# The activation of SwiGLU, turned between two matmuls: by transposing DMA of halfword planes instead of TensorE

## The chip, the cores and the metric

One core of one Trainium2 chip runs the whole program. The metric is the device time of one execution in microseconds (us), the median of several executions. The engines are named as in the profile: PE (TensorE, matmuls), ACT (ScalarE), DVE (VectorE), POOL (GpSimd) and SP (SyncE, which here only issues DMA). Sixteen DMA engines move data between DRAM and the on-chip memory (SBUF); matmul results land in PSUM, in 8 banks.

## The reference

One layer of a decoder: 256 tokens, width 2048, all in float32. The change lies in the feed-forward part, the last but one of the layer's parts.

```python
D_MODEL = 2048; SEQ = 256; D_FF = 5632
...
x = x + rms_norm(merged @ w_out[layer], g_mix_post[layer])

h = rms_norm(x, g_ffn_pre[layer])
gate, up = jnp.split(h @ w_gate_up[layer], 2, axis=-1)
x = x + rms_norm((jax.nn.silu(gate) * up) @ w_down[layer], g_ffn_post[layer])

ple_gate = jax.nn.sigmoid(rms_norm(x, g_ple_pre[layer]) @ w_ple_gate[layer])
...
```

`silu(gate) * up` is "the activation": 256 tokens by 5632 channels. It comes out of the first matmul with tokens on the partitions, and the second matmul needs it with channels on the partitions, so it has to be turned (transposed) in between.

## The kernel before

**Products.** A float32 product is made of three matmuls of a faster type: each operand is split into a high part, made by a copy on ACT (`wh` of a weight, `hi` of an activation), and the rest, made by a subtraction on DVE (`wl`, `lo`). `terms` issues high by high, low by high and high by low. Some blocks of weights go by "quads": seven products in place of eight, with sums of weights (`t`, made on DVE) and sums of activations (`sides`, split into `shi` and `slo`).

**The feed-forward part.** The 256 tokens are two chunks `c` of 128. `swiglu(j)` makes block `j` (of `NJ` = 11, 512 channels each) of gate and up from `w_gate_up`; `ev_g` and `ev_u` take the sums out of PSUM, and the product of silu(gate) and up is a tile `t` (named `u`, or `sg` for block 0) of 128 tokens by 512 channels. `gated(c, j, t)` then turns it: four PE transposes into a PSUM bank (`misc<-ident,u`), one ACT copy to SBUF (`actT<-misc`), and a store to a DRAM scratch tile `actd[c][j]` from the SP queue. There are 22 such tiles of 256 KB.

The second matmul takes the channels in five groups of blocks (`KGROUPS`), once for the left half of the output's columns and once, backwards, for the right half (`DOWN`). `act_parts(pair, gi)` prepares a group's activation while PE works on the group before: `load(j)` fetches both chunks of a block from `actd` by DMA from the POOL queue, one block ahead of its use, and `split` makes `hi` and `lo` of each. Blocks are loaded again for the second half, except for the group at the turn: 40 loads in 9 groups.

**What sets the order.** Weights are loaded by SP into six buffers `raw`, in a fixed plan. Work beside the matmuls is written as generators ("chains"): each `yield` says after what or after how long the chain may go on, by the planner's own estimate of time, which advances with every matmul that is written. So the order of each engine's instructions is fixed when the program is built; at run time each engine goes through its own list in that order, and waits where an operand or a buffer isn't there. If a matmul is written and its `hi` and `lo` aren't, `hurry` writes the missing steps on the spot:

```python
def hurry(done):
    while not done():
        due, _, gen = heapq.heappop(waiting)
        step(gen, due)
```

Tiles live in 61 equal SBUF slots; `room(n)` holds a chain back until n of them are free. In the estimate, DMA transfers take no time of an engine; `act_parts` leaves 6.0 us between the first load of a group and its use. All recorded instructions carry line 181, that of the recording helper, so the profile's groups go by the tiles' names.

Of the kernel before, what the change touches and what calls it, by code (L numbers as in the profile page):

```python
# [13 lines left out]
F32 = mybir.dt.float32  # L14
F32R = mybir.dt.float32r
I32 = mybir.dt.int32
AF = mybir.ActivationFunctionType
ALU = mybir.AluOpType
AX = mybir.AxisListType

P = 128
D = 2048
NB = 512
DFF = 5632
NJ = DFF // NB
# [4 lines left out]

TABLES = (AF.Sigmoid, AF.Silu, AF.Exp, AF.Ln, AF.Sin)
TABLE_LOAD = 1.3
# [96 lines left out]
def block_kernel(ctx: ExitStack, tc: tile.TileContext, I, out: bass.AP):  # L129
# [24 lines left out]
    class InOrder:  # L154
# [20 lines left out]
        def __getattr__(self, name):  # L175
            f = getattr(self.engine, name)

            def call(o, *a, **kw):
                if name != "dma_start":
                    self.estimate(name, o, a, kw)  # L180
                return tc.keep_in_program_order(f(o, *a, **kw))  # L181

            return call

    V = InOrder(nc.vector, 0.07, 0.00105)
    A = InOrder(nc.scalar, 0.16, 0.0008)
    G, T, S = InOrder(nc.gpsimd, 0.9, 0.002), InOrder(nc.tensor, 0.0, 0.0), InOrder(nc.sync, 0.0, 0.0)
# [9 lines left out]
    def transpose(o, i, idn):  # L197
        clock[0] += SMALL
        T.transpose(o, i, idn)
# [29 lines left out]
    def nm(s):  # L229
        count[0] += 1  # L230
        return f"{s}_{count[0]}"
# [4 lines left out]
    def slot(s, shape=(P, NB), dt=F32):  # L236
        i = free_slots.popleft()
        t = slots.tile(list(shape), dt, tag=f"s{i}", name=nm(s))
        owner[id(t)] = i, t
        return t  # L240

    def free(*tiles):
        for t in tiles:
            free_slots.append(owner.pop(id(t))[0])

    def room(n):

        while len(free_slots) < n:
            yield 0.3
# [13 lines left out]
    def drop(ps):  # L263
        banks.append(bank_of.pop(id(ps))[0])
# [5 lines left out]
    def misc():  # L270
        while len(banks) < 3:
            yield 0.3
        return bank("misc")

    def act(o, i, f, **kw):
        return A.activation(o, i, f, **kw)

    def tt(o, a, b, op):
        return V.tensor_tensor(o, a, b, op)
# [12 lines left out]
    def cols(h, d=P):  # L292
        return slice(h * d, (h + 1) * d)
# [21 lines left out]
    def split_pair():  # L315
# [3 lines left out]
        if isinstance(raw, list):  # L319
            parts = [(slot("wh", dt=F32R), slot("wl", dt=F32R)) for j in range(2)]  # L320
            for (hi, lo), r in zip(parts, raw):
                act(hi, r, AF.Copy)
                tt(lo, r, hi.bitcast(F32), ALU.subtract)
            done = partial(free, *parts[0], *parts[1])
            free(*raw)
        elif len(in_pool) < SPLIT + 1:
            hi = wsplit.tile([P, 2, NB], F32R, tag="wh", name=nm("wh"))
            lo = wsplit.tile([P, 2, NB], F32R, tag="wl", name=nm("wl"))
            act(hi, raw, AF.Copy)
            tt(lo, raw, hi.bitcast(F32), ALU.subtract)  # L330
            parts, done = [(hi[:, j, :], lo[:, j, :]) for j in range(2)], in_pool.popleft
            in_pool.append(k)
        else:
            parts = [(slot("wh", dt=F32R), slot("wl", dt=F32R)) for j in range(2)]
            for j in range(2):
                act(parts[j][0], raw[:, j, :], AF.Copy)
            for j in range(2):
# [4 lines left out]
    def parts_of_pair():  # L342

        w, k, col, raw, _ = loaded.popleft()
        if len(in_pool) <= SPLIT:
            hi = wsplit.tile([P, 2, NB], F32R, tag="wh", name=nm("wh"))
            lo = wsplit.tile([P, 2, NB], F32R, tag="wl", name=nm("wl"))
            in_pool.append(k)
            act(hi, raw, AF.Copy)
            yield  # L350
            tt(lo, raw, hi.bitcast(F32), ALU.subtract)
            parts, done = [(hi[:, j, :], lo[:, j, :]) for j in range(2)], in_pool.popleft
        else:
            parts = [(slot("wh", dt=F32R), slot("wl", dt=F32R)) for j in range(2)]
            for j in range(2):
                act(parts[j][0], raw[:, j, :], AF.Copy)
            yield
# [271 lines left out]
    def lookup(groups):  # L629
        def there(g):  # L630
            return g in groups if isinstance(groups, dict) else len(groups) > g and groups[g] is not None

        def f(k):
            hurry(lambda: there(k // 4))
            hi, lo = groups[k // 4]
            return hi[:, k % 4, :], lo[:, k % 4, :]
        f.groups = groups
        return f
# [17 lines left out]
    def transpose4(src):  # L656
        ps = yield from misc()
        for i in range(4):
            transpose(ps[:, cols(i)], src[:, cols(i)], ident)
        return ps  # L660

    def split(src, to, at):

        yield from room(2)
        hi = slot("hi", (P, 4, P), F32R)
        lo = slot("lo", (P, 4, P), F32R)
        hf = hi.rearrange("p c t -> p (c t)")
        act(hf, src, AF.Copy)
        yield A
        tt(lo.rearrange("p c t -> p (c t)"), src, hf.bitcast(F32), ALU.subtract)  # L670
        to[at] = hi, lo
# [70 lines left out]
    dram = ctx.enter_context(tc.tile_pool(name="dram", bufs=1, space=bass.MemoryType.DRAM))  # L742
# [64 lines left out]
    sinks = amask[:, 256:272]  # L807
    posi = cst.tile([P, 2], I32, name="posi")

# [223 lines left out]
    def hgrn_core(c, g):  # L1033
# [55 lines left out]
        def scores(lev):  # L1089
# [22 lines left out]
            if lev < 5:  # L1112
                V.copy_predicated(
                    right(sc),
                    cmask[:, cols(lev, 64)].rearrange("p (n w) -> p n w", w=w).unsqueeze(1)
                    .broadcast_to([P, 4, nb, w]).bitcast(I32),
                    pv.rearrange("p h (n w) -> p h n w", w=w))
# [446 lines left out]
    collect, _, apply_and_scale = post(gp)  # L1564
# [37 lines left out]
        block("w_out", K16, n * NB, mL, ev_out(n), LAG * (n == 3), n == 3, mixed_used if n == 3 else None)  # L1602


    actd = [[dram.tile([P, NB], F32, name=nm("actd")) for _ in range(NJ)] for _ in range(2)]
    stored, parts, sides, down_sides = [set(), set()], [], {}, {}
    h2T = [lookup(n.groups) for n in norm2]

    def gated(c, j, t):

        pa = yield from transpose4(t)
        free(t)
        yield T
        at = slot("actT")
        act(at, pa, AF.Copy)
        drop(pa)
        S.dma_start(actd[c][j], at)
        free(at)
        stored[c].add(j)

    def swiglu(j):
        sg, us = [None, None], []

        def ev_g(c, ps):
            def f():
                if j in BY_QUADS and SEVEN:
                    t = yield from total(us, 0, c, ps)
                    yield V
                    act(t, t, AF.Silu, scale=norm2[c].r)
                else:  # L1630
                    yield from norm2[c].ready()
                    t = slot("sg")
                    act(t, ps, AF.Silu, scale=norm2[c].r)
                    drop(ps)
                sg[c] = t
            chain(f())

        def ev_u(c, ps):
            def f():
                if j in BY_QUADS and SEVEN:  # L1640
                    t = yield from total(us, 1, c, ps)
                    while sg[c] is None:
                        yield 0.3
                    yield sg[c]
                    stt(t, t, norm2[c].r, sg[c], ALU.mult, ALU.mult)
                    free(sg[c])
                else:
                    while sg[c] is None:
                        yield 0.3
                    t = sg[c]  # L1650
                    stt(t, ps, norm2[c].r, t, ALU.mult, ALU.mult)
                    drop(ps)
                yield V
                yield from gated(c, j, t)
            chain(f())

        if j in BY_QUADS:
            order = quads_of_block(j)
            if j == NJ - 1:
                parts.extend(act_parts(0, 0))  # L1660
            by_quads("w_gate_up", [j * NB, DFF + j * NB], order, h2T, sides, [[acc(), acc()] for _ in range(2)],
                     {"left": sum(seven for _, seven in order)}, us, evac=lambda n, c, ps: (ev_g, ev_u)[n](c, ps))
            return
        block("w_gate_up", K16, j * NB, h2T, ev_g, LAG * (j == 0))
        depth[0] = SPLIT
        if j == 0:
            in_quads[0] = True
            chain(sides_of(ALL, lambda c: norm2[c].groups, sides))
        block("w_gate_up", K16, DFF + j * NB, h2T, ev_u)

    def act_parts(pair, gi):
        js = KGROUPS[gi]
        hurry(lambda: all(j in stored[c] for c in range(2) for j in js))
        parts = [{}, {}]

        def load(j):
            ts = [slot("act"), slot("act")]
            for c in range(2):
                G.dma_start(ts[c], actd[c][j])
            return ts  # L1680

        def f():
            yield from room(2)
            ts = load(js[0])
            yield 6.0
            for at, j in enumerate(js):
                yield from room(2)
                now, ts = ts, load(js[at + 1]) if at + 1 < len(js) else None
                for c in range(2):
                    yield from split(now[c], parts[c], j)  # L1690
                    yield 0.5
                for i in range(2):
                    wanted = 2 * j + i in SEVEN_DOWN[pair] or (gi == 4 and 2 * j + i in SEVEN_DOWN[1])
                    if wanted and 2 * j + i not in down_sides:
                        a = [t.rearrange("p (c t) -> p c t", c=4)[:, 2 * i + k, :] for t in now for k in range(2)]
                        down_sides[2 * j + i] = yield from in_place_of_quad(*a)
                    yield 0.5
                free(*now)
                yield 2.0
        chain(f())  # L1700
        return parts

# [9 lines left out]
    collect, apply, _ = post(gp)  # L1712
    for at, (pair, gi) in enumerate(DOWN):
# [3 lines left out]
        js = KGROUPS[gi]  # L1717
# [137 lines left out]
```

## Time and profile before

| | |
|---|---|
| median of 3 runs | 1489.03 us (1486.18 to 1490.61) |
| profiled execution, its own time | 1489.56 us |
| its span on the core | 1487.5 us |
| PE busy | 1469.5 us, 99% |
| DVE busy | 1239.9 us, 83% |
| ACT busy | 888.9 us, 60% |
| POOL busy | 62.9 us, 4% |
| DMA | 314.59 MB, mean 211 GB/s |
| granted clock | 0.997 |

Around the span lie 2.06 us of the profiled execution. The product with `w_gate_up` runs from about 705 to 1152 us of the span, the one with `w_down` from there to about 1361 us; its activation is loaded and split from 1102 us on. In a line of the profile, "tile<-tiles" are outputs and inputs by the program's names, "x22" is a count, and "[2.66 <-PE acc L181]" is how long the engine was idle ahead of the row and who ended that.

### The profile page before, as it was taken

The numbers are of one execution on the slowest core, as the hardware profiler recorded it, in microseconds if no ns is written. First come the engines' busy times: TensorE is split into PE (matmuls) and PEld (weight loads), VectorE is DVE, ScalarE is ACT, GpSimd is POOL, SyncE is SP. The second block draws the span as 40 slices with busy tenths as digits, with TensorE's granted clock in tenths as the row PEclk, the third lists the DMA queues.
The fourth block names the chain that finished last, engine by engine and source line by source line (L and its number), as shares of the span: only waits on it lengthen the run. The fifth ranks groups of instructions, "written<-read, shape, count | busy, mean of one in ns | idle before, by whom it ended". The sixth has DMA issues, their size and how long they took to land.

```text
span 1487.5 us, 19958 instructions
## 1 busy us (share of the span) xinstructions
PE 1469.5 (99%) x6838; PEld 1216.3 (82%) x6838; DVE 1239.9 (83%) x2043; ACT 888.9 (60%) x1417; POOL 62.9 (4%) x107
## 2 busy tenths in 40 slices
PE   9999999999999999999999999999999999999997
PEld 6888888888887888888888888888888887888885
DVE  6878958755999867977899999999988899997773
ACT  7755655566666645665655666565655666575661
POOL 2100000000000100000000000000000000010000
PEclk9999999999999999999999999999999999999998
DMA  9754544345576856866756676576677678797551
GB/s 342 257 188 155 171 141 128 114 128 170 184 240 227 309 185 201 272 227 199 252 182 219 205 238 213 174 230 206 215 239 268 214 252 270 214 336 260 192 188 56
DMA packets 159557, 314.59 MB, mean 211 GB/s; under 512 B 11072, under 2 KB 11520, under 8 KB 159456
## 3 DMA queue, kind: packets, MB, share of 16 engines
q1 hardware_dynamic: 153024, 293.38, 61.0%
q0 software_dynamic: 6256, 19.88, 3.7%
q8 instruction: 53, 0.87, 0.2%
q14 instruction: 48, 0.39, 0.1%
q10 hardware_dynamic: 176, 0.07, 0.0%
HBM read 298.08 MB, written 15.21 MB: 211 GB/s over the span
## 4 chain that ended last, share of the span: by engine, by line
PE 64%; DVE 4%; issue 2%; DMA 1%; ACT 1%; DVEq 0%; POOLq 0%; POOL 0%; ACTq 0%
PE acc L181 63%; DVE wl L181 2%; PE misc L181 1%; DVE u L181 1%; ACT wh L181 1%; DVE t L181 1%; DMA raw<-in_w_in 1%; DMA raw<-in_w_down 0%; DMA raw<-in_w_gate_up 0%; DVE eg L181 0%; DVE slo L181 0%; DVE lo L181 0%; ACT hi L181 0%; DVE sides L181 0%; DVE s L181 0%
## 5 line engine op out<-in xcount | busy, mean ns | idle before, releaser
L181 PE MATMUL acc<-wh,hi 128*128 128x512 f32 x1769 | 700.2, 396 | 3.6 <-DVE u L181 2.4
L181 DVE TENSOR_TENSOR wl<-raw,wh 128x1024 fp32r<-128x1024 f32 (+1 forms) x606 | 595.7, 1007 | 115.4 <-ACT wh L181 113.8
L181 PE MATMUL acc<-wl,hi 128*128 128x512 f32 x1769 | 690.0, 390 | 0.0
L181 PE MATMUL acc<-wh,lo 128*128 128x512 f32 x1769 | 688.9, 389 | 0.0
L181 ACT ACTIVATE wh<-raw 128x1024 fp32r<-128x1024 f32 (+1 forms) x606 | 514.3, 883 | 239.8 <-PE acc L181 101.6
L181 PEld LDWEIGHTS acc<-wl,hi 128*128 128x128 f32 x1769 | 332.0, 188 | 71.2 <-DVE wl L181 1.1
L181 PEld LDWEIGHTS acc<-wh,hi 128*128 128x128 f32 x1769 | 332.3, 188 | 70.6 <-DVE u L181 3.2
L181 PEld LDWEIGHTS acc<-wh,lo 128*128 128x128 f32 x1769 | 332.5, 188 | 66.6 <-issue 0.2
L181 ACT ACTIVATE wh<-t 128x512 fp32r<-128x512 f32 x236 | 145.6, 628 | 106.6 <-DVE t L181 85.9
L181 DVE TENSOR_TENSOR wl<-t,wh 128x512 fp32r<-128x512 f32 x236 | 152.2, 683 | 0.5 <-PE acc L181 0.5
L181 DVE TENSOR_TENSOR u<-acc,u 128x512 f32<-128x512 f32 x132 | 86.3, 684 | 18.8 <-PE acc L181 17.6
L181 PE MATMUL acc<-wh,shi 128*128 128x512 f32 x236 | 91.9, 390 | 1.2 <-ACT shi L181 1.2
L181 PE MATMUL acc<-wh,slo 128*128 128x512 f32 x236 | 91.9, 390 | 0.2 <-DVE slo L181 0.2
L181 PE MATMUL acc<-wl,shi 128*128 128x512 f32 x236 | 91.8, 389 | 0.0
L181 DVE TENSOR_TENSOR t<-raw,t 128x512 f32<-128x512 f32 x118 | 81.1, 687 | 3.7
L181 PEld LDWEIGHTS acc<-wh,shi 128*128 128x128 f32 x236 | 44.3, 188 | 10.8 <-ACT shi L181 1.6
L181 PEld LDWEIGHTS acc<-wh,slo 128*128 128x128 f32 x236 | 44.3, 188 | 9.7 <-DVE slo L181 0.5
L181 PEld LDWEIGHTS acc<-wl,shi 128*128 128x128 f32 x236 | 44.3, 188 | 9.2
L181 POOL DMA_DIRECT2D act<-actd x40 | 21.4, 538 | 601.9 <-DVE wl L181 402.4
L181 DVE TENSOR_TENSOR t<-raw,raw 128x512 f32<-128x512 f32 x59 | 40.3, 684 | 3.9 <-DMA raw<-in_w_gate_up 1.9
L181 DVE TENSOR_TENSOR t<-raw 128x512 f32<-128x512 f32 x59 | 40.3, 684 | 0.0
L181 DVE TENSOR_TENSOR lo<-act,hi 128x512 fp32r<-128x512 f32 x40 | 27.2, 684 | 8.1 <-ACT hi L181 8.0
(214 smaller groups left out, 852.1 us busy)
## 6 DMA issues: line engine op xcount, KB each, us to landing
raw<-in_w_gate_up SPq DMA_DIRECT2D x176, 512.0 KB, 4.6
raw<-in_w_in SPq DMA_DIRECT2D x152, 512.0 KB, 4.3
raw<-in_w_down SPq DMA_DIRECT2D x88, 512.0 KB, 5.5
raw<-in_w_out SPq DMA_DIRECT2D x32, 512.0 KB, 5.5
raw<-in_w_ple_gate SPq DMA_DIRECT2D x32, 512.0 KB, 5.1
act<-actd POOLq DMA_DIRECT2D x40, 256.0 KB, 5.6
raw<-in_w_attn_branch SPq DMA_DIRECT2D x16, 512.0 KB, 5.2
raw<-in_w_hgrn_branch SPq DMA_DIRECT2D x16, 512.0 KB, 5.1
```

Source lines behind the costliest of these rows:

```text
L181: return tc.keep_in_program_order(f(o, *a, **kw))
```

## The change

The PE transposes, their PSUM banks and the ACT copy out of PSUM go. In their place `gated` has ACT copy the float32 tile, seen as 1024 halfwords (16 bits), into two planes: all low halfwords, then all high ones (`halves`). The planes go to `actd`, untransposed. On the way back, `load` issues a transposing DMA of 16-bit elements from the ACT queue, 128 by 1024 halfwords into 128 x 8 x 128 (`turned`): four squares of 128 by 128 for each plane, each turned. A second ACT copy (`act<-turned`) interleaves the two planes again into a float32 tile, on which `split` then works as before.

```diff
             def call(o, *a, **kw):
-                if name != "dma_start":
+                if not name.startswith("dma_start"):
                     self.estimate(name, o, a, kw)
...
-    actd = [[dram.tile([P, NB], F32, name=nm("actd")) for _ in range(NJ)] for _ in range(2)]
+    actd = [[dram.tile([P, 2 * NB], U16, name=nm("actd")) for _ in range(NJ)] for _ in range(2)]
...
+    def halves(t):
+
+        return t.bitcast(U16).rearrange("p (n two) -> p two n", two=2)
+
     def gated(c, j, t):

-        pa = yield from transpose4(t)
+        at = slot("halves", (P, 2 * NB), U16)
+        act(at.rearrange("p (two n) -> p two n", two=2), halves(t), AF.Copy)
         free(t)
-        yield T
-        at = slot("actT")
-        act(at, pa, AF.Copy)
-        drop(pa)
         S.dma_start(actd[c][j], at)
         free(at)
         stored[c].add(j)
...
                 yield V
-                yield from gated(c, j, t)
+                gated(c, j, t)
...
         def load(j):
-            ts = [slot("act"), slot("act")]
+            ts = [slot("turned", (P, 8, P), U16) for _ in range(2)]
             for c in range(2):
-                G.dma_start(ts[c], actd[c][j])
+                A.dma_start_transpose(ts[c], actd[c][j])
             return ts
...
             for at, j in enumerate(js):
                 yield from room(2)
-                now, ts = ts, load(js[at + 1]) if at + 1 < len(js) else None
+                turned, ts = ts, load(js[at + 1]) if at + 1 < len(js) else None
+                now = []
                 for c in range(2):
+                    yield from room(3)
+                    now.append(slot("act"))
+                    act(halves(now[c]), turned[c].rearrange("p (two c) t -> p two (c t)", two=2), AF.Copy)
+                    free(turned[c])
+                    yield A
                     yield from split(now[c], parts[c], j)
```

Numbers at the end of a name count the tiles in the order in which the code makes them, over all engines.

PE, at the end of a block of `w_gate_up`, before: the activation `u` of both chunks is turned between two matmuls.

```order
L181 MATMUL acc_10653<-wh_10468,lo_6378 128x512
L181 MATMUL acc_10653<-wl_10469,hi_6377 128x512
L181 MATMUL misc_10669<-ident,u_10188 128x128 x4
L181 MATMUL misc_10674<-ident,u_10186 128x128 x4
L181 MATMUL acc_10654<-wh_10468,hi_6507 128x512
L181 MATMUL acc_10654<-wh_10468,lo_6508 128x512
```

After the change no row of that kind (`misc` from `u` or `sg` of a block) is left on PE: 88 transposes are gone, and the `acc` rows follow each other.

ACT, at the first group of loads (about 1107 to 1113 us of the span), before; the loads themselves stand on POOL, in a list of their own.

```order
L181 ACTIVATE wh_10642<-t_10640 128x512
L181 ACTIVATE actT_10679<-misc_10669 128x512
L181 ACTIVATE actT_10685<-misc_10674 128x512
L181 ACTIVATE u_10604<-u_10604,rest_6726 128x512
L181 ACTIVATE u_10602<-u_10602,rest_6592 128x512
L181 ACTIVATE hi_10709<-act_10649 128x512
```

The same place on ACT after:

```order
L182 ACTIVATE wh_10581<-t_10579 128x512
L182 DMA_TRANSPOSE turned_10583<-actd_6422 128x8x128
L182 DMA_TRANSPOSE turned_10584<-actd_6433 128x8x128
L182 DMA_TRANSPOSE turned_10624<-actd_6423 128x8x128
L182 DMA_TRANSPOSE turned_10625<-actd_6434 128x8x128
L182 ACTIVATE u_10537<-u_10537,rest_6726 128x512
L182 ACTIVATE u_10535<-u_10535,rest_6592 128x512
L182 ACTIVATE act_10637<-turned_10583 128x2x512
L182 ACTIVATE halves_10643<-u_10536 128x1024
```

The loads have moved into ACT's list, and the copy that waits for the first of them stands two instructions behind them.

ACT, at the last block that is prepared (about 1345 to 1357 us), before: between one `hi` of the activation and the next stand four or five other copies.

```order
L181 ACTIVATE hi_13113<-act_13042 128x512
L181 ACTIVATE u_13119<-acc_12332 128x512
L181 ACTIVATE wh_13127<-raw_13037 128x512
L181 ACTIVATE wh_13129<-raw_13037 128x512
L181 ACTIVATE wh_13144<-raw_13053 128x1024
L181 ACTIVATE hi_13152<-act_13043 128x512
```

The same place after:

```order
L182 ACTIVATE act_13152<-turned_12914 128x2x512
L182 ACTIVATE hi_13156<-act_13152 128x512
L182 ACTIVATE wh_13172<-raw_13071 128x1024
L182 ACTIVATE wh_13184<-raw_13098 128x1024
L182 ACTIVATE act_13190<-turned_13081 128x2x512
L182 ACTIVATE hi_13192<-act_13190 128x512
L182 ACTIVATE act_13202<-turned_13082 128x2x512
L182 ACTIVATE hi_13204<-act_13202 128x512
```

Copy and split of one tile stand back to back, as `hurry` writes them; and on PE the matmuls that read these tiles follow without the distance that they had:

```order
L182 MATMUL acc_12175<-wl_12949,hi_13130 128x512
L182 MATMUL acc_12176<-wh_12948,hi_13156 128x512
L182 MATMUL acc_12176<-wh_12948,lo_13157 128x512
L182 MATMUL acc_12176<-wl_12949,hi_13156 128x512
L182 MATMUL acc_12176<-wh_12948,hi_13156 128x512
L182 MATMUL acc_12176<-wh_12948,lo_13157 128x512
L182 MATMUL acc_12176<-wl_12949,hi_13156 128x512
L182 MATMUL acc_12175<-wh_12969,hi_13192 128x512
L182 MATMUL acc_12175<-wh_12969,lo_13193 128x512
```

A chunk's activation is read for six matmuls, then comes the next tile. Counted in the order in which the code writes instructions for all engines, 11 of the 40 `lo` tiles now stand 2 matmuls ahead of the first matmul that reads them; before, none stood closer than 14.

More of the change, by code (lines that the diff above doesn't have):

```diff
@@ L16 @@
 I32 = mybir.dt.int32
+U16 = mybir.dt.uint16
 AF = mybir.ActivationFunctionType
```

## The prediction

> **What bounds the kernel now.** I read the page's engine lines first, then the busy time by stretches for the two stages that the change touches, then PE's waits.
>
> ```profile
> span 1487.5 us, 19958 instructions
> PE 1469.5 (99%) x6838; PEld 1216.3 (82%) x6838; DVE 1239.9 (83%) x2043; ACT 888.9 (60%) x1417; POOL 62.9 (4%) x107
> ```
> ```profile
> 720.00:1165.00 445.00, 444.54 (x2001) 367.63 (x2000) 415.64 (x604) 267.39 (x400) 5.38 (x10) 1.00 0.67 215
> ```
> ```profile
> 1100.00:1360.00 260.00, 258.56 (x1152) 213.71 (x1151) 233.38 (x343) 162.74 (x247) 21.38 (x40) 1.00 0.77 257
> ```
> ```profile
> PE acc L181 <- ACT shi L181: 1.2, 1, 1.2
> PE acc L181 <- DVE slo L181: 0.2, 1, 0.2
> ```
>
> The columns of the two stretches are length, then busy time of PE, PE's weight loads, DVE, ACT and POOL, then clock, DMA share and GB/s. PE is busy for 444.54 of 445 us while the activation is made, and for 258.56 of 260 while it is loaded, split and used; the last rows are all that PE waits for in the second. So PE sets the time: a microsecond taken off PE is gained, and any wait of PE is lost whole. DVE stands next (93% and 90%), then ACT (60% and 63%). What counts is whether ACT and DVE stay ahead of PE after the change.
>
> **Off PE: the transposes.** They are seen between two matmuls:
>
> ```profile
> 1109.47 0.39 PE L181 MATMUL acc<-wl,hi 128*128 128x512 f32 x1
> 1109.70 1.03 PE L181 MATMUL misc<-ident,u 128*128 128x128 f32 x8
> 1110.50 0.48 PE L181 MATMUL acc<-wh,hi 128*128 128x512 f32 x1
> 1110.82 0.40 PE L181 MATMUL acc<-wh,lo 128*128 128x512 f32 x1
> 1111.05 0.40 PE L181 MATMUL acc<-wl,hi 128*128 128x512 f32 x1
> ```
>
> Matmuls start 0.23 us apart (1110.82 to 1111.05). Eight transposes hold the start of the next matmul for 1110.50 - 1109.70 = 0.80 us, and the step behind it is 0.32 in place of 0.23: 0.89 us for both chunks of a block, 11 blocks, **-9.8 us**, all of it on the path. DVE then has its 415.64 us in 435 (96%). Nothing is added to it there, so I take no loss.
>
> **On ACT, making the activation.** 22 copies out of PSUM become 22 copies of 1024 halfwords. The nearest row for these is the copy of 1024 elements:
>
> ```profile
> L181 ACT ACTIVATE actT<-misc x22: 578/597/602, 731.5 to 1160.9; 128x512 f32<-128x512 f32 x22
> ```
> ```profile
> L181 ACT ACTIVATE wh<-raw 128x1024 fp32r<-128x1024 f32 x63 | 65.2, 1053 | 61.6 <-DMA raw<-in_w_down 37.2 <-PE acc L181 24.3
> L181 ACT ACTIVATE hi<-act 128x512 fp32r<-128x512 f32 x40 | 24.3, 617 | 1.3 <-PE acc L181 1.3
> ```
>
> 22 x (1.053 - 0.597) = 10 us more on ACT, of which 6 fall into the second stretch (2.7 us). ACT is idle for 178 of 445 us here; cost 0. The stores stay on SP at the same place, and wait for a copy as before.
>
> **On ACT, loading it.** 40 copies `act<-turned` of 1024 halfwords: 40 x 1.053 = 42 us. 40 DMA issues come over from POOL, where they cost nobody anything (it was 4% busy). No row shows the issue of a transposing transfer. The nearest rows are the two plain issues of ACT's own queue, 0.45 and 0.49 us, and for the upper end the slowest issue of an activation's store on SP, 1182 ns:
>
> ```profile
> 0.74 0.45 ACTq L181 DMA_DIRECT2D ident<-in_c_ident  x1
> 1.21 0.49 ACTq L181 DMA_DIRECT2D grow<-in_g_mix_pre  x1
> ```
> ```profile
> L181 SPq DMA_DIRECT2D actd<-actT x22: 319/338/1182, 732.1 to 1161.5; - x22
> ```
>
> Neither end is nearer by its kind, since a plain issue names rows of 2 KB and this one pieces of them; I take the middle, 0.8 us: 32 us (19 to 47). ACT's work in the second stretch becomes 162.7 + 42 + 32 + 2.7 = 239.5 us (226 to 255) of 257 (three of the PE pairs fall into it): 93%, or 88 to 99%.
>
> **The new wait.** Before, POOL waited for the slots and the loads alone. Now the loads stand in ACT's list, at ACT's own place, and behind them in that list stand all the weights' copies `wh`, for which DVE waits, and then PE. The first load of each of the 9 groups stands 27 matmuls (6.1 us) ahead of its first copy. In the trace, ACT came by the same two places like this, at the first and the second group:
>
> ```profile
> 1106.76 0.64 ACT L181 ACTIVATE wh<-t 128x512 fp32r<-128x512 f32 x1
> 1110.34 1.10 ACT L181 ACTIVATE actT<-misc 128x512 f32<-128x512 f32 x2 [2.94 <-PE misc L181]
> 1111.33 1.32 ACT L181 ACTIVATE u<-u,rest 128x512 f32<-128x512 f32 x2
> 1112.56 0.62 ACT L181 ACTIVATE hi<-act 128x512 fp32r<-128x512 f32 x1
> ```
> ```profile
> 1153.47 1.32 ACT L181 ACTIVATE u<-u,rest 128x512 f32<-128x512 f32 x2
> 1154.70 0.61 ACT L181 ACTIVATE wh<-raw 128x512 fp32r<-128x512 f32 x1
> 1155.39 0.64 ACT L181 ACTIVATE wh<-t 128x512 fp32r<-128x512 f32 x1
> 1155.93 1.05 ACT L181 ACTIVATE wh<-raw 128x1024 fp32r<-128x1024 f32 x1
> 1156.88 0.61 ACT L181 ACTIVATE hi<-act 128x512 fp32r<-128x512 f32 x1
> ```
>
> From the end of the row ahead of the loads to the first `hi` it was 5.2 us (1107.4 to 1112.6) and 2.1 us (1154.8 to 1156.9). A transfer of the same bytes took, from issue to landing:
>
> ```profile
> DMA to landing us min/median/max: 3.8/5.6/7.9
> ```
>
> With 5.6 us and the mean distance of 3.7, ACT stands for 1.9 us at each of 9 places, 17 us; with 3.8, nearly none; with 7.9 and 2.1, 52. That brings ACT's demand to 256 of 257 us (226 to 307): just at its limit, with nothing left to catch up with.
>
> **What PE then waits for.** The order shows it: 11 `lo` tiles, in 7 places (both chunks late in 4 of them), stand 2 matmuls (0.45 us) ahead of their reader, because the chain of a block has become longer by a copy per chunk and by the room that it waits for, and `hurry` writes the rest on the spot. Before, the closest stood 14 ahead, and even there little was left:
>
> ```profile
> 1214.70 0.68 DVE L181 TENSOR_TENSOR lo<-act,hi 128x512 fp32r<-128x512 f32 x1
> 1215.30 0.69 DVE L181 TENSOR_TENSOR wl<-t,wh 128x512 fp32r<-128x512 f32 x1
> 1215.90 1.29 DVE L181 TENSOR_TENSOR lo<-act,hi 128x512 fp32r<-128x512 f32 x2
> ```
> ```profile
> 1217.13 0.39 PE L181 MATMUL acc<-wh,hi 128*128 128x512 f32 x1
> 1217.37 0.40 PE L181 MATMUL acc<-wh,lo 128*128 128x512 f32 x1
> ```
>
> The second of the pair of `lo` ended at 1217.19 and was read at 1217.37, although it stood 17 matmuls (3.9 us) ahead of that read: DVE ran 3.7 us later than the order. Tiles that stand 0.45 us ahead make PE wait about 3.2 us by this row. The other way to price it is the chain itself, as if ACT began it just when PE needs it: copy 1.05, `hi` 0.62, `lo` 0.68, less 0.45, that is 1.9 us. Where the second chunk is late too, ACT needs 1.67 us more for it while PE has six matmuls (1.36 us) to do: 0.3 us. 7 x 1.9 + 4 x 0.3 = 14.5 us by the chain, 7 x 3.2 + 1.2 = 23.6 by the row, 0 if ACT runs well ahead of PE. I take 16, near the chain, since PE's own waits give ACT and DVE time to recover between places that lie 5 to 60 us apart.
>
> **Sum.** -9.8 + 16 = +6.2 us on the profiled execution's 1489.56 us: 1495.8. That execution lies 0.5 us above the median of the runs (1489.03), so I forecast **1495.5 us**. With PE's waits at 6 to 28 us this case alone gives 1485 to 1508.
>
> **Rivals.**
>
> *ACT and DVE stay ahead (faster).* For it: PE's cover of split weights is large. ACT once stood for 7.19 us and PE did not wait at all there:
>
> ```profile
> 1183.82 1.06 ACT L181 ACTIVATE wh<-raw 128x1024 fp32r<-128x1024 f32 x1 [7.19 <-DMA raw<-in_w_down]
> ```
>
> With an issue of 0.47 us and a landing within 4, ACT has 226 us of work in 257 and may be some microseconds ahead at the late places. Then PE loses 0 to 5 us and the time is 1479 to 1484. Against it: that cover is one of weights, and the late tiles are the activation's, which have none. It decides at PE waits of 9.8 us in all, where gain and loss are equal.
>
> *ACT becomes the bound (slower still).* If the issue holds ACT for 1.18 us and the landing is 5.6, ACT's demand is 255 + 17 = 272 of 257 us: 15 us more than PE can hide, beside the 14.5 of the chains: 1489.0 - 9.8 + 29.5 = 1508.7. With 7.9 at every first load it is 307, and 1489.0 - 9.8 + 50 = 1529 by ACT's demand alone. Against it: the two plain issues of that queue are less than half as long. It decides where ACT's demand passes 257 us.
>
> *The DMA engines become the bound (slowest).*
>
> ```profile
> q1 hardware_dynamic: 153024, 293.38, 61.0%
> q0 software_dynamic: 6256, 19.88, 3.7%
> ```
>
> A packet of the first queue carries 1.92 KB and takes 0.610 x 16 x 1487.5 / 153024 = 95 ns; one of the second 3.18 KB and 0.037 x 16 x 1487.5 / 6256 = 141 ns. A square of 128 halfwords has rows of 256 bytes, so a transfer would be 1024 pieces, 64 per engine. If a piece takes as long as a packet of the first queue, a transfer holds all engines for 6.1 us and 40 of them for 243 us, in place of 40 x 0.76 = 30 us. The stretch has 0.77 x 260 = 200 us of DMA work; it would have 413, 156 more than PE's 257: 1489 - 9.8 + 156 = 1635. Against it: the two packets lie on a line of some 25 ns and 0.036 ns per byte, by which a piece takes 34 ns and 40 transfers 87 us: 257 us of DMA work, just what PE needs. It decides at 34 ns per piece. [...]
>
> *The change doesn't do what it says.* The order excludes it: the PE rows are gone, and 40 transposing issues stand on ACT.
>
> **Chances.** Forecast 0.48, ahead of PE 0.24, ACT as bound 0.18, DMA as bound 0.08, something else near the old time 0.02. Below 1484.6 or above 1493.5 (0.3%) is about what a measurement of this kernel tells from no change. Slower: 0.31 of the forecast's 0.48, with 0.18 and 0.08, is 0.57. The same: 0.15 of the forecast, 0.02 of the faster case and the 0.02, together 0.19. Faster: 0.22 and 0.02, 0.24. The range of 1480 to 1521 leaves out the DMA case (0.08), the upper end of ACT as bound (0.06) and the lower end of the faster case (0.04).
>
> **What the profile after would show.** Right: no `misc<-ident,u` on PE; the first stretch shorter by about 9 us and still filled by PE; in the second, PE waits of 10 us and more, on `lo<-act,hi` and `hi<-act`, at `lo` tiles of the late blocks; ACT above 85% busy there. Wrong: PE as full as before (then the faster case), or PE waiting for `wl` and `wh` of weights (then ACT or DMA is the bound; the landing time of `turned<-actd` and the DMA share tell which). The forecast falls if ACT runs some 3 us ahead of PE at the late places, or if a transposing issue holds its queue far longer than 1.2 us.

## The result and the profile after

The changed kernel takes 1550.68 us (median of four executions, 1546.59 to 1553.8) beside 1489.21 of the kernel before: a ratio of 1.0415 [1.0387, 1.0443], 61.5 us slower. The forecast was 1495.5 us with a range of 1480 to 1521; the sign was right, the time lies far outside.

The page of the changed kernel (its recording line is 182 now), and PE's clock in fortieths of the span:

```profile
span 1552.0 us, 19730 instructions
PE 1484.4 (96%) x6750; PEld 1219.6 (79%) x6750; DVE 1243.1 (80%) x2044; ACT 944.4 (61%) x1458; POOL 40.9 (3%) x67
PE   9999999999999999999999999999998789677997
PEclk9999999999999999999999999999999799888999
```

Its two stretches, in the same columns as before:

```profile
720.00:1165.00 445.00, 445.00 (x1965) 368.59 (x1964) 418.04 (x607) 283.70 (x408) 0.00 (x0) 1.00 0.71 217
1100.00:1360.00 260.00, 224.78 (x921) 180.24 (x919) 192.60 (x285) 165.41 (x226) 0.00 (x0) 0.92 0.83 205
```

The first stretch is as full of PE work as it was, at full clock. The loss lies in the second: PE works 224.78 of 260 us, not 258.56, and its clock is 0.92, not 1.00. What PE waits for, and what ACT waits for (total, times, longest):

```profile
PE acc L182 <- ACT hi L182: 30.1, 8, 7.2
PE acc L182 <- DVE lo L182: 11.9, 9, 4.7
PE acc L182 <- ACT shi L182: 7.0, 2, 4.8
PE acc L182 <- DVE slo L182: 3.8, 4, 2.8
```
```profile
ACT act L182 <- issue: 24.8, 8, 7.6
ACT wh L182 <- issue: 13.2, 8, 3.4
ACT wh L182 <- DMA raw<-in_w_down: 26.3, 8, 10.8
```

PE waits 52.8 us for the parts of the activation (`shi` and `slo` are those of its sums), where it waited 1.4. ACT, which makes `hi`, stood before its own next instruction with nothing to wait for that the profile shows, "issue". The transfers themselves, and the timeline of ACT at one such place (rows with ACTq are its DMA issues):

```profile
L182 ACTq DMA_TRANSPOSE turned<-actd x40: 1247/1334/6515, 1101.2 to 1405.0; - x40
L182 ACT ACTIVATE act<-turned x40: 1312/1354/1387, 1107.9 to 1428.4; 128x1024 uint16<-128x1024 uint16 x40
DMA to landing us min/median/max: 3.4/8.4/17.6
```
```profile
1315.15 6.51 ACTq L182 DMA_TRANSPOSE turned<-actd  x1
...
1316.42 2.00 ACT L182 ACTIVATE wh<-raw 128x1024 fp32r<-128x1024 f32 x2
1321.69 4.26 ACTq L182 DMA_TRANSPOSE turned<-actd  x1
1326.00 2.53 ACT L182 ACTIVATE act<-turned 128x1024 uint16<-128x1024 uint16 x2 [7.58 <-issue]
...
1331.83 0.61 ACT L182 ACTIVATE hi<-act 128x512 fp32r<-128x512 f32 x1
```
```profile
1332.50 0.79 PE L182 MATMUL acc<-wh,hi 128*128 128x512 f32 x1 [7.15 <-ACT hi L182]
```
```profile
L182 ACT ACTIVATE act<-turned 128x1024 uint16<-128x1024 uint16 x40 | 53.6, 1352 | 32.9 <-issue 24.8 <-PE acc L182 7.0 <-DMA actd<-halves 1.2
```

ACT finishes two copies of weights at 1318.4 and does nothing until 1326.0, while two issues hold its queue one after the other, 6.51 and 4.26 us. PE gets its `hi` from there at 1332.4, and has waited 7.15 us for it. The 40 issues on the timeline, from 1101.15 to 1404.99, add up to 88 us, but not all of that stops ACT: the two copies of 1316.42 ran while the issue of 1315.15 was under way. ACT's idle time that the profile puts down to issues ahead of `act`, `wh` and `u` is 42.8 us, where it was 8.9 before. Four more stops, of 15.3 us together, are put down to PE but end within 0.1 us of the end of an issue. So about 49 of the 88 us stop ACT. The last row is all that ACT stood ahead of the 40 copies: 32.9 us, of which 1.2 end with a transfer.

Behind a stop like this PE's matmuls look as follows, and the clock by 10 us:

```profile
1216.56 0.39 PE L182 MATMUL acc<-wh,slo 128*128 128x512 f32 x1
1216.79 0.39 PE L182 MATMUL acc<-wl,shi 128*128 128x512 f32 x1
1222.97 0.79 PE L182 MATMUL acc<-wh,hi 128*128 128x512 f32 x1 [5.80 <-ACT hi L182]
...
1224.38 0.63 PE L182 MATMUL acc<-wl,hi 128*128 128x512 f32 x1
1224.80 0.63 PE L182 MATMUL acc<-wh,hi 128*128 128x512 f32 x1
1225.23 0.63 PE L182 MATMUL acc<-wh,lo 128*128 128x512 f32 x1
```
```profile
1220.00:1230.00 10.00, 5.00 (x9) 2.90 (x10) 5.68 (x11) 7.57 (x11) 0.00 (x0) 0.50 0.55 142
1230.00:1240.00 10.00, 10.00 (x39) 8.08 (x39) 7.81 (x13) 4.58 (x8) 0.00 (x0) 0.86 0.59 114
```

Ahead of the wait matmuls start 0.23 us apart, behind it 0.42 to 0.43, and the granted clock of those 10 us is 0.50. So a wait like this costs more than its own length. It isn't so behind every wait: in the same kernel the matmuls stay slow behind a wait of 2.81 us (1178.19) and not behind one of 2.82 (1428.57).

### The profile page after: what moved, and what is told of

It is laid out like the page before. It is cut to its first block, busy times and chain, and to the rows that moved or that the text cites. A ratio compares the mean times of both kernels' runs of the same rounds, so it can differ in the third digit from the quotient of the medians.

```text
span 1552.0 us, 19730 instructions
## 1 busy us (share of the span) xinstructions
PE 1484.4 (96%) x6750; PEld 1219.6 (79%) x6750; DVE 1243.1 (80%) x2044; ACT 944.4 (61%) x1458; POOL 40.9 (3%) x67
## 3 DMA queue, kind: packets, MB, share of 16 engines
q10 hardware_dynamic: 42416, 10.56, 5.8%
## 5 line engine op out<-in xcount | busy, mean ns | idle before, releaser
L182 PEld LDWEIGHTS acc<-wh,hi 128*128 128x128 f32 x1769 | 335.8, 190 | 106.1 <-ACT hi L182 33.9
L182 ACT ACTIVATE act<-turned 128x1024 uint16<-128x1024 uint16 x40 | 53.6, 1352 | 32.9 <-issue 24.8
```

## The experiments

Ratios are to the kernel before on the same chip, with their 95% intervals.

**Without the turning.** From the kernel before, the transposes and the copies out of PSUM are taken away; the activation is stored and loaded as it is.

```diff
-        pa = yield from transpose4(t)
+        S.dma_start(actd[c][j], t)
         free(t)
-        yield T
-        at = slot("actT")
-        act(at, pa, AF.Copy)
-        drop(pa)
-        S.dma_start(actd[c][j], at)
-        free(at)
```

> The kernel before without its 88 PE transposes and the 22 copies out of PSUM: the activation is stored as it is and loaded plain from POOL (the turning is left out). It measures the first term of the sum by itself: 9.8 us less, 1476 to 1481 us. If the transposes were hidden on PE or DVE can't follow a faster PE, 1483 to 1489 us.

1479.79 us, 0.9945 [0.9927, 0.9963]: 8.2 us less (5.5 to 10.9). PE's waits for the activation stay at 2.9 us. The term for the transposes holds. All that the change adds is to be counted from here, 1480.

**Plain loads, from POOL and from ACT.** Everything else of the changed kernel stays (its order and its copies of halfwords), and nothing is turned.

```diff
-                A.dma_start_transpose(ts[c], actd[c][j])
+                G.dma_start(ts[c].rearrange("p a b -> p (a b)"), actd[c][j])
```

> The changed kernel with its order, its copies and its SBUF tiles, but the 40 loads are plain DMA issued from POOL, as before the change; the planes come back unturned (this part of the computation is left out). Theory A (ACT is held by the issue of the transposing transfers, 1.3 us and up to 6.5 us each): most of the loss goes, 1490 to 1502 us, PE's waits fall from 53 to under 20 us. Theory B (the recorded order: activation tiles written 2 matmuls ahead of their reader, plus copies of 1.35 us): the loss stays, 1520 to 1550 us, PE's waits 30 us or more. Theory C (pieces of 256 bytes fill the DMA engines, so weights and activation land late): 1490 to 1505 us like A, and weights land in 5.5 us or less; e2 and e3 tell A from C.

> As the run before it, but the 40 plain loads are issued from ACT, at the place where the changed kernel issues its transposing ones (the turning is left out). Theory A: a plain issue holds ACT for 0.5 us in place of 1.3 to 6.5, so 1492 to 1508 us, within 8 us of the run with POOL. Theory B: 1520 to 1550 us. Theory C: as the run with POOL, within 5 us. If it is the place in ACT's list as such that costs (ACT waits there for slots and landings), it comes out 15 us or more above the run with POOL.

From POOL 1509.24 us, 1.0141 [1.0125, 1.0158]; from ACT 1513.72, 1.0171 [1.0156, 1.0186]. PE's waits with POOL, and the issues on ACT:

```profile
PE acc L182 <- ACT hi L182: 15.0, 7, 3.9
PE acc L182 <- DVE lo L182: 5.4, 9, 2.2
PE acc L182 <- DVE slo L182: 0.3, 1, 0.3
```
```profile
L182 ACTq DMA_DIRECT2D turned<-actd x40: 326/390/617, 1103.4 to 1366.5; - x40
```

So 21 us of the loss, 29 above the kernel without turning, come without any transposing transfer, with 20.7 us of PE waits; that a plain load stands in ACT's list adds 4.5 us. The transposing transfer in its place adds 36 (1.0415 less 1.0171). The time from POOL lies above the ranges of theories A and C and below that of B, the one from ACT above that of A and below that of B: none of them explains the loss alone.

**The transposing loads from SP.** `A.dma_start_transpose` becomes `S.dma_start_transpose`.

> The changed kernel with its 40 transposing transfers issued from SP in place of ACT, nothing else changed. Theory A: ACT is free of the issues, 1500 to 1520 us; what is left is weights' loads that stand behind the issues on SP. Theory B: 1535 to 1550 us, since order and copies stay. Theory C: 1545 to 1565 us, as the pieces stay and the weights' loads now also wait behind them.

1525.17 us, 1.025 [1.0235, 1.0265], outside the ranges of all three theories. Of the 41 us between the changed kernel and the plain loads from POOL (1.0415 less 1.0141), 24.5 go with the issue's place on ACT. The issues are no shorter on SP, but there they hold up only other transfers:

```profile
L182 SPq DMA_TRANSPOSE turned<-actd x40: 1231/2522/4903, 1097.4 to 1383.1; - x40
DMA to landing us min/median/max: 3.4/5.8/9.9
```

The other 16 us lie between this kernel and the plain loads from POOL. At least two things differ there: the transfers land later (5.8 us in place of 4.9), and their issues stand in the queue from which the weights are loaded. ACT's waits for weights of `w_down` are 35.6 us here and 16.2 there. Plain loads from SP, which would tell the two apart, weren't tried.

**Half the pieces.** Only the high plane is turned, from ACT and from SP; a copy of the same length puts it into both halves of each word.

```diff
-            ts = [slot("turned", (P, 8, P), U16) for _ in range(2)]
+            ts = [slot("turned", (P, 4, P), U16) for _ in range(2)]
-                A.dma_start_transpose(ts[c], actd[c][j])
+                A.dma_start_transpose(ts[c], actd[c][j][:, NB:])
```

> The changed kernel with half of each transposing transfer: only the high plane of halfwords is turned (512 halfwords of a row, 32 pieces of 256 bytes per engine instead of 64), and the copy behind it writes that plane into both halves of each word, so the low halves of the activation are left out of the result; the copy's length and the order stay. Theory (the cost goes by pieces: their descriptors are written while the issue holds ACT): the issue falls from 1.33 to about 0.75 us, the landing from 8.4 to about 5.5, PE waits 30 to 40 us instead of 53, 1518 to 1535. Rival (the cost is one per transposing transfer, whatever its size): issue and landing stay, 1543 to 1553.

> The same half transfers, issued by SP instead of ACT, so that ACT's list holds no issue. With the whole transfers from SP it was 1525, 16 us above the plain loads of the same order (1509). Theory (those 16 us are the later landing, which goes by pieces): half of them go, 1513 to 1519. Rival (they are a fixed cost of each transposing transfer): 1522 to 1527.

From ACT 1525.13 us, 1.0251 [1.0231, 1.0271]; from SP 1516.43, 1.0192 [1.0165, 1.0218]. Both times are where the cost by pieces put them; from ACT the landing is 5.6 us, as expected, and PE's waits are 29.1, just below the range given. But the issue isn't 0.75 us:

```profile
L182 ACTq DMA_TRANSPOSE turned<-actd x40: 1204/1232/1301, 1100.5 to 1375.0; - x40
```
```profile
L182 SPq DMA_TRANSPOSE turned<-actd x40: 1188/1216/3137, 1098.7 to 1375.7; - x40
DMA to landing us min/median/max: 2.5/4.5/9.3
```

The issue has a floor that hardly falls with the size, 1.25 us for the whole and 1.20 for half from ACT; what goes by size is the tail. With 64 pieces per engine issues took up to 6.5 us, with 32 these rows of ACT end at 1.30, and the sum on the timeline falls from 88 to 50 us. Half of the expectation (a cost by pieces) fits the tail, the rival's half (a cost per transfer) the floor. That descriptors are written while an issue holds its queue, as the expectation has it, is shown by no run.

**The order.** One `yield A` between the copy of halfwords and the split is taken out, so that 2 instead of 11 `lo` tiles stand two matmuls ahead of their readers; with the transposing loads from ACT, from SP, and with plain loads from POOL.

```diff
                     free(turned[c])
-                    yield A
                     yield from split(now[c], parts[c], j)
```

> The changed kernel without the planner's pause between the interleaving copy of a chunk and its split: copy and high part stand back to back on ACT, which changes the order only. Of the 40 low parts 2, not 11, then stand 2 matmuls ahead of their reader, and 5 to 12 us are usual in the second pass. Theory B: PE's waits on the activation fall by half or more, 1500 to 1525 us. Theory A: no instruction and no issue is gone, 1540 to 1551 us. Theory C: 1545 to 1551 us.

> Both of the above: plain loads from POOL (the turning is left out) and no pause between copy and split. What is left against the kernel before: 40 interleaving copies of 1.35 us and 22 of 1.04 us on ACT, no transposes on PE. If order and transposing transfers are all that costs, PE's waits fall under 6 us and it is the gain with little taken off: 1480 to 1490 us. If the copies themselves fill ACT: 1493 to 1505 us, with PE waits above 10 us.

> Transposing transfers issued from SP, and no pause between copy and split. If the two losses add, 1525 - 15 = 1510 us (1503 to 1516). If with ACT free the order has more to spare, 1490 to 1503 us. If the pieces of 256 bytes on the DMA engines are what is left, 1515 us and more, with weights landing later than 5.5 us.

From ACT 1535.34 us, 1.0313 [1.0278, 1.0348]; from SP 1506.48, 1.0127 [1.0114, 1.014]; plain 1495.17, 1.005 [1.0037, 1.0062]. Each is 14 to 18 us below its partner with the changed order. From ACT the time lies between the ranges of the theories, and PE's waits fall by a quarter (52.8 to 39.8 us), not by half; from SP it is where the two losses add; with plain loads it is where the copies themselves were to cost. There PE still waits:

```profile
PE acc L182 <- DVE lo L182: 8.7, 6, 2.6
PE acc L182 <- ACT hi L182: 1.2, 3, 0.9
```

So the late places are real, and they aren't all: some 15 us stay above the kernel without turning.

**Short copies.** In the last kernel, plain with POOL, both copies of 1024 halfwords become copies of 512 words.

```diff
-        act(at.rearrange("p (two n) -> p two n", two=2), halves(t), AF.Copy)
+        act(at.bitcast(F32), t, AF.Copy)
...
-                    act(halves(now[c]), turned[c].rearrange("p (two c) t -> p two (c t)", two=2), AF.Copy)
+                    act(now[c], turned[c].rearrange("p a b -> p (a b)").bitcast(F32), AF.Copy)
```

> The plain loads from POOL without the yield behind the copy (1495.2), and both kinds of copies made plain ones of 512 f32 elements (about 0.6 us instead of 1.35 and 1.04): what is stored isn't split into planes, and nothing is turned. The order of the instructions stays. Theory (what is left above the kernel without turning, 15 us, is ACT's time in the copies, since ACT and DVE have no slack in this stage): most of it goes, 1481 to 1487. Rival (it is the place of the copy in the chain that counts, a step more behind each load, whatever its length): 1491 to 1496.

1482.26 us, 0.9963 [0.995, 0.9976], inside the theory's 1481 to 1487. The copies take 0.62 us instead of 1.35, and PE's waits for `lo` are gone:

```profile
L182 ACT ACTIVATE act<-turned x40: 611/617/622, 1104.2 to 1351.7; 128x512 f32<-128x512 f32 x40
```
```profile
PE acc L182 <- ACT shi L182: 3.1, 1, 3.1
PE acc L182 <- DVE lo L182: 0.3, 1, 0.3
```

But the order didn't stay, as the expectation had it. The planner estimates a copy on ACT at 0.16 us and 0.0008 for each element, so a copy of half the elements changes what it writes when: written out, no `lo` is left 2 matmuls ahead of its reader, and the closest stands 8 ahead. So 13 us (1.005 less 0.9963) go with the length of the copies, directly and by the order that the planner makes of it; the two weren't tried apart. That the chain has a step more costs 2.7 us or nothing: the intervals of this kernel and of the one without turning overlap.

**The copies on POOL.** In the kernel with loads from SP and without the yield, `act(halves(...))` becomes `G.tensor_copy(halves(...))`. This one computes the whole.

> The transposing loads from SP without the yield (1506.5), and the 40 copies that put the halfwords together on POOL instead of ACT; POOL has nothing else to do here. It computes the whole. [...] Theory (ACT's own time in issue and copies makes PE wait): ACT gets 54 us back, PE waits at a few late places only, 1486 to 1496. Rival (the length of the chain load, copy, hi, lo counts at the late places, and POOL's copy is longer): 1504 to 1520.

1526.54 us, 1.0267 [1.0247, 1.0286], 20 us worse than with the copies on ACT and beyond even the rival's range. A copy takes POOL 1.9 us on the mean (76.9 us of its busy time in 40), beside 1.35 on ACT, and once 6.94, and the late places wait for it:

```profile
L182 POOL COPY act<-turned x40: 1315/1760/6942, 1100.7 to 1384.0; 128x1024 uint16<-128x1024 uint16 x40
```
```profile
PE acc L182 <- DVE lo L182: 20.5, 10, 4.3
```

ACT got some 53 us back (it is busy for 155.88 us between 1150 and 1440, in place of 208.74), and the time rose all the same. Why it rose isn't shown by this run, since more than the engine of the copy changed. The planner estimates this copy on POOL at 2.9 us, and in the order that it then writes 6 `lo` tiles, not 2, stand 2 matmuls ahead of their readers. And DVE, which makes `lo`, is busy for 1271.7 us in place of 1241.4 with about as many instructions. Its 40 `lo` take 0.76 us on the mean, where they take 0.69 with the copies on ACT; beside a copy of POOL one took 1.76, later one 0.69:

```profile
1209.63 4.83 POOL L182 COPY act<-turned 128x1024 uint16<-128x1024 uint16 x3 [17.34 <-PE acc L182]
```
```profile
1213.19 1.76 DVE L182 TENSOR_TENSOR lo<-act,hi 128x512 fp32r<-128x512 f32 x1
1222.75 0.69 DVE L182 TENSOR_TENSOR lo<-act,hi 128x512 fp32r<-128x512 f32 x1
```

The longer copy, its place in POOL's list, the order and the slower DVE weren't tried apart.

**Filling the waits.** In the changed kernel 126 products with a zero matrix, 14 at each of nine places where a tile was read late, keep PE at work there. They add 126 x 0.227 = 28.6 us of PE work.

```diff
+        while fill[0]:
+            mm(ps, zero, wh, t=0.0, start=start, stop=False)
+            start, fill[0] = False, fill[0] - 1
```

> The changed kernel with 14 matmuls by a zero tile (3.2 us at full clock; they add zero to the sums) written on PE ahead of the reads of an activation that isn't there yet, 9 places, 126 in all. They take PE's time, but PE mostly waits there. Theory D (each wait also lowers PE's clock for some microseconds after it, which costs about 20 of the 62 us): with the waits filled the clock stays up, 1528 to 1543 us, although PE does more. Without such an effect: 1550 us or more, since what outlasts a wait is added.

1551.16 us, 1.0428 [1.041, 1.0446], the same as the changed kernel: the expectation missed. The waits fell from 52.8 to 35.0 us, less than the fill cost. At filled places they shrank, at 1222 from 5.80 us to 2.03, but some of the longest stood where no fill was written, and stayed or grew. The first of these rows is from the changed kernel, the second, at the same place, from this one:

```profile
1359.73 0.79 PE L182 MATMUL acc<-wh,hi 128*128 128x512 f32 x1 [6.92 <-ACT hi L182]
1360.65 0.80 PE L182 MATMUL acc<-wh,hi 128*128 128x512 f32 x1 [9.79 <-ACT hi L182]
```

The slow matmuls are seen at another such place, late in both kernels (2.22 us there, 2.40 here):

```profile
1200.12 0.79 PE L182 MATMUL acc<-wh,shi 128*128 128x512 f32 x1 [2.40 <-ACT shi L182]
...
1205.70 0.63 PE L182 MATMUL acc<-wh,shi 128*128 128x512 f32 x1
...
1206.78 0.40 PE L182 MATMUL acc<-wh,hi 128*128 128x512 f32 x1
```

After this stop the matmuls stay 0.43 us apart from 1201 to 1206, then go back to 0.23: fifteen steps of 0.2 us too much, some 3 us. By itself the run doesn't separate waits from clock, and with several of the longest waits unfilled it is a weak test of theory D. It helps in the accounts below.

**The accounts.** Each kernel's span is set against the 1480.0 us of the one without turning. W is PE's waits for `hi`, `lo`, `shi` and `slo` (2.9 us in that one); the rest is the span's difference less that of W (and less 28.6 us for the fill). The next column is the span times what its mean granted clock lacks of 1, less the same of the kernel without turning (4.4 us). The last is how much longer PE was busy than in the kernel without turning, whose line is this (again less the 28.6 us):

```profile
PE 1460.9 (99%) x6750; PEld 1208.9 (82%) x6750; DVE 1240.0 (84%) x2044; ACT 876.7 (59%) x1396; POOL 63.0 (4%) x107
```

| kernel | span | W | rest | lost clock | PE busy |
|---|---|---|---|---|---|
| changed | 1552.0 | 52.8 | 22 | 31 | 24 |
| changed, waits filled | 1553.8 | 35.0 | 13 | 19 | 15 |
| no yield | 1531.4 | 39.8 | 15 | 20 | 17 |
| loads from SP | 1523.2 | 31.7 | 14 | 17 | 16 |
| copies on POOL | 1524.4 | 34.2 | 13 | 15 | 15 |
| one plane, ACT | 1521.4 | 29.1 | 15 | 15 | 17 |
| one plane, SP | 1517.1 | 24.3 | 16 | 18 | 15 |
| plain, ACT | 1513.0 | 24.6 | 11 | 14 | 13 |
| plain, POOL | 1511.1 | 20.7 | 13 | 12 | 12 |
| no yield, SP | 1506.5 | 20.2 | 9 | 11 | 11 |
| no yield, plain | 1490.3 | 10.8 | 2 | 5 | 4 |
| short copies | 1480.5 | 3.4 | 0 | 2 | 1 |

Besides the fill, each of these kernels has the same 6750 matmuls, so the last column is how much slower they ran. It matches the rest within 3 us in every kernel: what W leaves unexplained is slower matmuls. The rest also rises and falls with the lost clock. The lost clock is mostly the larger, and more so where W is large; a clock that is low during a wait would do that, since nothing is lost there (in the changed kernel it was 0.67 from 1217.20 to 1222.90, a stretch without a matmul). So the changed kernel's 72 us over 1480 are 50 us of waits and 22 us of slower matmuls, which go with the clock. This is an accounting over kernels; no run held the clock and the waits apart.

In steps, each by its ratio times 1488: the transposes taken off -8; one step more in the chain +2.7 (short copies); the copies' length, with the order that follows from it, +13 (no yield, plain); the late places that the `yield` makes +14 (plain, POOL); transposing loads from SP instead of plain ones from POOL +16; their issue on ACT +24.5. The sum is +62.

## Why the prediction was wrong, and where it was right

*What bounds the kernel, and the first term: right.* PE sets the time, and the transposes were worth 8.2 us (5.5 to 10.9) where 9.8 was forecast. In the changed kernel itself the stores show the stretch shorter by about as much, 420.8 us from first to last in place of 429.4:

```profile
L182 SPq DMA_DIRECT2D actd<-halves x22: 356/357/422, 732.7 to 1153.5; - x22
```

*Making the activation, cost 0: right.* The first stretch stayed full.

*Loading it, the issue: the step that failed.* The forecast chose 0.8 us between 0.47 and 1.18, from plain issues. It is 1.33 us in the median, above the upper end, and 2.2 in the mean, since a transposing issue that comes soon after another is often held for 2 to 6.5 us: 88 us in all instead of 32. And the forecast took it as load that ACT hides; in the trace a held issue stops ACT ahead of the copy that PE needs next. Taken off ACT's list, that is 24.5 us. The copy was priced at 1.05 us by a copy of 1024 words; with halfwords written to every second place it takes 1.35, 54 us instead of 42. Was it then the rival "ACT becomes the bound"? The forecast's own sum with these numbers is 162.7 + 54 + 88 + 2.7 = 307 us of ACT in 257, 50 more than PE can hide, and W is 50 us above the kernel without turning. That the two agree is luck: with the 49 us of issues that do stop ACT the sum is 268, 11 more than PE can hide. ACT is busy for 165 of the 260 us, 64% (issues aren't counted as busy), where the forecast had above 85, and PE waits 0.9 us for `wh`, the sign that the forecast had named for this rival. So the rival's condition came, an issue above 1.18 us, but not its mechanism: ACT isn't full, it is stopped at single places on the way to the next tile.

*The new wait.* Landing was taken as 5.6 us by the plain transfer; it was 8.4 in the median from ACT, and 5.8 from SP, so most of the excess isn't the transfer. The forecast had ACT stand some 17 us for it; of ACT's idle time ahead of the copies 1.2 us end with a transfer, and nearly all the rest with an issue.

*What PE then waits for.* For the late places the forecast took 16 us, near the chain. With the order and the copies alone (plain loads from POOL) W is 20.7, 19.3 more than before. By the forecast's formula with 1.35 us for the copy it is 7 x 2.2 + 4 x 0.6 = 17.8. The mechanism was right, and the size as a wait: taking the `yield` out took 10 us of W with it. As time, order and copies cost more, 29 us over the kernel without turning, since slower matmuls come on top. The sign of the forecast rests on this term and wasn't luck: without any transposing transfer the kernel is 21 us slower than before. What was missing is what the late issues add: W of 52.8.

*The sum.* Of the 55 us between 1495.5 and 1550.7, the issue's place on ACT is 24.5, the transposing loads from SP in place of plain ones are 16, for which the forecast had nothing, the late places and the copies are 13 (29 in place of 16), and the transposes 1.6.

*A term that wasn't there: the clock.* The forecast made a microsecond of waiting cost a microsecond. By the accounts it cost about 1.4 here. The rows of before gave no way to see that, since PE waited for 1.4 us only, at a clock of 0.997; but a forecast of tens of microseconds of waiting should have asked what the granted clock does behind a wait. The runs show no one answer: in the 10 us around the row at 1222.97, with 5.80 us idle ahead of it, it was 0.50; at 1200.12, in the kernel with filled waits, the matmuls were slow for some 6 us behind a wait of 2.40; and of the two waits of 2.8 us in the changed kernel one was followed by slow matmuls and one wasn't. From what length on a wait has this behind it isn't shown.

*The DMA engines as the bound: did not happen.* Its deciding price nearly did:

```profile
q1 hardware_dynamic: 153024, 293.38, 59.8%
q10 hardware_dynamic: 42416, 10.56, 5.8%
```

Queue 10 carries the turned pieces: 0.058 x 16 x 1552.0 / 42416 = 34 ns each, just the line's estimate. In the kernel without the yield, with the queue's share at 4.9%, it is 28. The share over the stretch is 0.83, so the engines weren't full on the mean. The eight squares of a transfer landed in 3.4 us at the fastest, and from SP the landing was near that of a plain load (5.8 us in the median, beside 4.9 from POOL). The issue wasn't near: 1.33 us in the median from ACT, beside 0.39 of a plain one from the same queue.

*What would show it wrong.* The forecast named the event, a transposing issue that holds its queue far longer than 1.2 us, and gave it no more than a part of 0.18, because the plain issues of that queue took half a microsecond.

No version tried that turns the whole activation came below the kernel before; the nearest is loads from SP without the yield, 1506.48 us.

## What to carry to other kernels

Here 40 transposing issues in ACT's list stopped ACT for about 49 us: before a new kind of transfer is put on an engine that feeds the bound, measure its issue alone and two in a row, and choose a queue whose engine nobody waits for. Chains whose end stood two matmuls ahead of the reader made the bound wait here, with ACT 64% busy: nine such tiles fewer were worth 14 to 18 us. So count the chain, not the engine's share of busy time. Where a planner orders instructions by estimated times, a shorter copy or another engine is another order too: compare the written orders before a difference is put down to length. When a forecast contains tens of microseconds of PE waits, price what the clock does after them as well: by the accounts a microsecond of waiting cost about 1.4 here.

## What was not expected of the hardware

- A transposing issue of 128 x 1024 halfwords cost its queue 1.23 us (SP) or 1.25 (ACT) at least, and up to 6.5 when another came shortly before; of half the size 1.19 at least, mostly without the tail. ACT ran copies that stood ahead of the next issue while one was under way: about 49 of 88 us stopped it. Why the second of two is held so long isn't shown. A plain issue of the same bytes from ACT's queue took 0.33 to 0.62.
- An ACT copy of 1024 halfwords took 1.35 us where it writes every second halfword and 1.04 where it reads every second; POOL took 1.9 us on the mean for the first.
- After some waits of a few microseconds PE's matmuls went at 0.43 us a step instead of 0.23; behind the wait at 1200.12 in the kernel with filled waits this lasted some 6 us. Of two waits of 2.8 us in the changed kernel one was followed by it and one wasn't.
- With such copies on POOL, DVE's subtraction of 128 x 512 took 0.76 us on the mean and 1.76 beside one of them, otherwise 0.69; in all DVE was busy for 30 us more.
